# Expert stage: the experts of the last 32 first keys computed densely, the others gathered by row

## The chip, the cores and the metric

The program runs on one core of one Trainium2 chip, in one launch. The metric is device time in microseconds (us); all arithmetic is float32 (parts of the GEMMs split a float32 operand in two). The core has a matrix engine (TensorE, in the profile PE, its weight loads PEld), three others for elementwise work (VectorE, DVE; ScalarE, ACT; GpSimd, POOL), SyncE (SP), which here only issues loads and stores, and sixteen DMA engines. POOL issues the gathers by row.

## The reference, cut to what matters

Two transformer blocks run one after the other on x of 256 tokens by 2048 columns. The change lies in the last part of the second block, a layer with 16,384 experts of one row each, of which every token uses 16 in each of 8 heads:

```python
q = (hf @ wq).reshape(T, PEER_HEADS, 2, PEER_DQ // 2)          # T = 256, 8 heads, 2 halves of 128
s = jnp.einsum('thpd,hpkd->thpk', q, keys)                     # 128 keys in each half
v1, i1 = lax.top_k(s[:, :, 0], 16);  v2, i2 = lax.top_k(s[:, :, 1], 16)
cand = v1[..., :, None] + v2[..., None, :]                     # 256 candidates
cidx = i1[..., :, None] * 128 + i2[..., None, :]               # expert = first key * 128 + second key
vals, pick = lax.top_k(cand, 16)
eidx, g = cidx[pick], softmax(vals)
act = gelu(einsum('td,thkd->thk', x_c, down[e_c])) * g_c       # down, up: 16384 x 2048
out = einsum('thk,thkd->td', act, up[e_c])                      # sum over heads and picks
```

The result is x + gt2 * out, where gt2 is one row of 2048 factors made from the conditioning vector. There are 256 * 8 * 16 = 32,768 picks. The first key of an expert is its index divided by 128.

## The kernel before, in words

Everything up to the expert stage is a chain of GEMMs with weights streamed in 1 MB pieces; nothing there changes. At its end, `hf` holds the normalized input, transposed (2048 features on 16 chunks of 128 partitions, 256 tokens along a row), `xN` the residual in the same layout, `htok` both token halves with tokens on partitions, and `gB` gt2 on all partitions. Instructions go through a helper that records all of them under line 94; the gathers are the exception (line 1600). From line 1528 on the order on each engine is chosen by a planner, which plays the program in a model of time; where it is free it follows the order of the code.

The stage's wq GEMM runs first. Work is then cut in 16 items: token half `qt` (128 tokens) by head `hd`. For each item:

- `route` (line 1557): two small matmuls against the keys, then top 16 of each half, top 16 of the 256 sums and their indices on DVE; result: expert indices `ei` and gates `g`, one row per token, one column per pick.
- `downs` (1603): for each of 16 picks, POOL gathers 128 rows of `down` (one per token, 8 KB each, 1 MB) into a tile `dn`, and DVE multiplies it with `htok` and sums it to one column of `dots`.
- the loop from line 1642: `cf` = gelu(dots) * g. For each pick, a gather of 128 rows of `up`, ACT puts the column of `cf` on a diagonal (`cdg`, 128 x 128), and four matmuls with it as weights add the 128 x 2048 tile, scaled by row, to four PSUM banks `acc`. The gathers of the next item's `dn` alternate with this item's `up`. The last two items do 14 of their rows on DVE instead (`side`).

After head 7 of a half, `acc` is multiplied by `gB`, added to the residual (`x3t`, tokens on partitions, made by 16 transposes) and stored.

Tiles of 8 KB per partition come from one pool of 14 (`unit`); `dn`, `htok`, `pq` (the wq result), `hf`, `xN`, `gB` and `keysT` share it. The tiles of `up` have eight buffers of another pool, in which GEMM weights were before. POOL issues gathers in order; each waits for its buffer.

Of the kernel before, what the change touches and what calls it, by code (L numbers as in the profile page):

```python
# [10 lines left out]
F32 = mybir.dt.float32  # L11
F32R = mybir.dt.float32r
I32 = mybir.dt.int32
# [7 lines left out]
P = 128  # L21
# [7 lines left out]
NCMP = 15  # L29


def _consts():
# [29 lines left out]
    for j in range(512):  # L62
# [7 lines left out]
    return {"cst_a": csta, "cst_b": cstb.astype(f), "cst_c": hot}  # L70
# [5 lines left out]
        "do": 5.0, "ro": 0.0, "nf": 3, "tail": 2}  # L76
# [3 lines left out]
def tile_kernel(ctx: ExitStack, tc: tile.TileContext, I, out):  # L80
# [1029 lines left out]
    def gt2_bcast():  # L1110
        acc = unit([P, D], "gB")
        yield from ada_acc(2, 5, acc)
        br = wp.tile([1, D], F32, name=nm("gb"), tag="W")
        SY.dma_start(br, I["ada_b_2"][:, 5 * D:6 * D])
        for q in range(4):
            sl = slice(512 * q, 512 * q + 512)
            ps = pmisc([P, 512], "gbp")
            T.matmul(ps, ones, acc[:, sl], start=True, stop=False)
            T.matmul(ps, ones[0:1, :], br[:, sl], start=False, stop=True)
            S.copy(acc[:, sl], ps)  # L1120
            yield 0.0
        mods["gB"] = acc

    queue_ada(*later[TUNE["nf"]:])
# [403 lines left out]
    pinned[0] = False  # L1528

# [16 lines left out]
    htok = [unit([P, D], "htok") for _ in range(2)]  # L1546
    down, upw = I["peer_down_2"][0], I["peer_up_2"][0]
    gB = mods["gB"]
# [7 lines left out]

    def route(qt, hd):
        ps = pmisc([P, 2, P], "ksc")
# [23 lines left out]
        ee = tiny([P, 2, 16], "ee")  # L1582
        for a in range(2):
            oh_ = scr([P, 16, 16], "oh")
            V.tensor_tensor(oh_, pf[:, 1 + a, :].unsqueeze(2).to_broadcast([P, 16, 16]),
                            iota16.unsqueeze(1).to_broadcast([P, 16, 16]), OP.is_equal)
            V.tensor_tensor(oh_, oh_, ixf[:, a, :].unsqueeze(1).to_broadcast([P, 16, 16]), OP.mult)
            V.tensor_reduce(ee[:, a, :], oh_, axis=AX.X, op=OP.add)
        V.scalar_tensor_tensor(ee[:, 0, :], ee[:, 0, :], 128.0, ee[:, 1, :], op0=OP.mult, op1=OP.add)
        ei = tiny([P, 16], "eid", I32)  # L1590
        V.tensor_copy(ei, ee[:, 0, :])
# [4 lines left out]
        V.tensor_scalar(g[:, 0:16], g[:, 0:16], g[:, 18:19], None, op0=OP.mult)  # L1596
        return ei, g

    def gather(rows_, table, idx):
        G.indirect_dma_start(out=rows_, out_offset=None, in_=table,  # L1600
                             in_offset=bass.IndirectOffsetOnAxis(ap=idx, axis=0))

    def downs(it):
        qt, hd, ei, g, dots = it
        for k in range(16):
            rt = unit([P, D], "dn")
            gather(rt, down, ei[:, k:k + 1])
            V.scalar_tensor_tensor(rt, rt, 1.0, htok[qt], op0=OP.mult, op1=OP.mult,
                                   accum_out=dots[:, k:k + 1])
            yield 2.2  # L1610

    def item(i):
        qt, hd = divmod(i, 8)
        ei, g = route(qt, hd)
        return qt, hd, ei, g, tiny([P, 16], "dots")

    def by_token():
        yield from hf_shift()
        for t in range(2):
            yield from tokens(hf, htok[t], t)  # L1620
# [6 lines left out]
    for nn in (256, 256, 512, 512, 512):  # L1627
# [6 lines left out]
        if c0 == 0:  # L1634
            dgen.append(downs(items[0]))
            stream.append(dgen[0])
# [3 lines left out]
    x3t = unit([P, D], "x3t")  # L1640
    side = None
    for i in range(16):
        qt, hd, ei, g, dots = items[i]
        if hd == 0:
            acc = [pacc_([P, 512], "pe") for _ in range(3)] + [pmisc([P, 512], "pe")]
        if i + 2 < 16:
            items.append(item(i + 2))
        cf = tiny([P, 16], "cf")
        S.activation(cf, dots, AF.Gelu)
        V.tensor_mul(cf, cf, g[:, 0:16])  # L1650
        nxt = downs(items[i + 1]) if i + 1 < 16 else iter(())
        for k in range(16):
            next(nxt, None)
            rt = rot_tile("up")
            gather(rt, upw, ei[:, k:k + 1])
            if i >= 16 - TUNE["tail"] and k % 2 == 0 and k < 14:

                if side is None:
                    side = unit([P, D], "side")
                    V.tensor_scalar(side, rt, cf[:, k:k + 1], None, op0=OP.mult)  # L1660
                else:
                    V.scalar_tensor_tensor(side, rt, cf[:, k:k + 1], side, op0=OP.mult, op1=OP.add)
                continue
            dg = scr([P, P], "cdg")
            S.activation(dg, ident, AF.Copy, scale=cf[:, k:k + 1])
            for n in range(4):
                T.matmul(acc[n], dg, rt[:, 512 * n:512 * n + 512], start=(hd == 0 and k == 0),
                         stop=(hd == 7 and k == 15), skip_group_check=True)
        for _ in nxt:
            pass  # L1670
        if hd == 5:
            for _ in tokens(xN, x3t, qt):
                pass
        if hd == 7:
            if side is not None:
                V.tensor_mul(side, side, gB)
                V.tensor_add(x3t, x3t, side)
            for n in range(4):
                sl = slice(512 * n, 512 * n + 512)
                o = scr([P, 512], "o")  # L1680
                V.tensor_mul(o, acc[n], gB[:, sl])
                V.tensor_add(o, o, x3t[:, sl])
                SY.dma_start(out[0, qt * P:(qt + 1) * P, sl], o)
# [24 lines left out]
```

## Time and profile before

| | |
|---|---|
| median of 3 runs | 3374.34 us (3374.03 to 3379.35) |
| the profiled execution | 3373.42 us, span from first to last instruction 3371.5 us |
| mean granted clock of PE | 0.938 |
| busy in the span: PE, DVE, ACT, POOL | 88%, 68%, 30%, 24% |
| gathers of `dn` and of `up` | 256 each |
| moved in all | 1068.19 MB, 538.26 MB of it on POOL's queue |

The profile is of one execution. Busy shares are of the whole span: three fifths of it, up to about 2050 us, are GEMMs with PE nearly full, and the expert stage comes after. A row of a group gives line, engine, operation, the tile written and those read, the count, then the busy time together, the mean of one instruction, the idle time of its engine just before, and what ended it.

### The profile page before, as it was taken

To read this page: it belongs to the slowest core of one execution; us is meant where nothing else is said; L and a number is where in the kernel's file an instruction comes from. 1 tells how busy PE (TensorE), PEld (TensorE's weight loads), DVE (VectorE), ACT (ScalarE), POOL (GpSimd) and SP (SyncE) were. 2 spreads that over 40 slices of the span, in tenths; PEclk is the share of its full clock that TensorE was granted. 3 is DMA by queue.
4 is the path that set the end of the run, shared out by engine and by line. 5 is a ranking of instruction groups with operands and counts; after the bars stand their busy time and mean duration, and the time that the engine had idled before them with its cause. 6 is when DMAs were issued, how large, how long until landed. Compare 5 with 4: busy or idle time off the path is not lost.

```text
span 3371.5 us, 44165 instructions
## 1 busy us (share of the span) xinstructions
PE 2971.9 (88%) x18020; PEld 2298.6 (68%) x18020; DVE 2302.0 (68%) x3363; ACT 1024.8 (30%) x1364; POOL 793.1 (24%) x540
## 2 busy tenths in 40 slices
PE   6899999999999999999999997877787678677777
PEld 2687889999999999999999997433333233223333
DVE  7687779876778778765876659655655566664735
ACT  1323433444444444444346653111111101111100
POOL 1000000000000000000000003666665566664654
PEclk8899999999999999999999998988888889888888
DMA  9866567876899989874783438999999999999998
GB/s 367 301 218 218 200 236 243 307 264 216 294 332 330 325 320 325 320 250 161 264 270 121 147 113 321 416 421 422 422 421 421 421 420 422 421 421 405 422 393 360
DMA packets 280401, 1068.19 MB, mean 317 GB/s; under 512 B 27428, under 2 KB 36039, under 8 KB 189573
## 3 DMA queue, kind: packets, MB, share of 16 engines
q1 hardware_dynamic: 202370, 524.35, 44.5%
q0 software_dynamic: 74752, 538.26, 38.7%
q10 hardware_dynamic: 3076, 2.76, 0.3%
q8 instruction: 141, 2.31, 0.3%
q14 instruction: 62, 0.51, 0.0%
HBM read 1063.19 MB, written 2.11 MB: 316 GB/s over the span
## 4 chain that ended last, share of the span: by engine, by line
PE 64%; DMA 24%; DVE 5%; issue 4%; POOL 3%; ACT 0%; SPq 0%; POOLq 0%; DVEq 0%; ACTq 0%
PE ga L94 48%; DMA up<-in_peer_up_dram,eid 12%; DMA dn<-in_peer_down_dram,eid 11%; PE pe L94 6%; PE gb L94 2%; DMA aw<-in_w_ada_dram 2%; POOL up L1600 2%; POOL dn L1600 2%; DVE dn L94 2%; PE adap L94 1%; PE bu L94 1%; PE rms L94 1%; PE yp L94 1%; PE o L94 1%; PE sc L94 0%
## 5 line engine op out<-in xcount | busy, mean ns | idle before, releaser
L94 PE MATMUL pe<-up,cdg 128*128 128x512 f32 x1936 | 920.7, 637 | 310.1 <-DMA up<-in_peer_up_dram,eid 189.1
L94 PEld LDWEIGHTS pe<-up,cdg 128*128 128x128 f32 x1936 | 390.1, 205 | 833.1 <-issue 621.2
L1600 POOL DMA_INDIRECT dn<-in_peer_down_dram,eid x256 | 394.5, 1541 | 2246.6 <-DVE g L94 1998.0
L94 DVE TENSOR_TENSOR wl<-w,wh 128x2048 fp32r<-128x2048 f32 (+2 forms) x304 | 680.6, 2239 | 316.8 <-ACT wh L94 265.4
L94 ACT ACTIVATE wh<-w 128x2048 fp32r<-128x2048 f32 (+2 forms) x304 | 570.0, 1875 | 882.3 <-PE ga L94 738.1
L94 DVE SCALAR_TENSOR_TENSOR dn<-dn,htok 128x2048 f32<-128x2048 f32 x256 | 583.1, 2288 | 326.2 <-DMA dn<-in_peer_down_dram,eid 325.7
L1600 POOL DMA_INDIRECT up<-in_peer_up_dram,eid x256 | 385.6, 1506 | 274.5 <-PE pe L94 98.8
L94 DVE SCALAR_TENSOR_TENSOR acc<-aw,cT,acc 128x2048 f32<-128x2048 f32 x105 | 246.3, 2346 | 22.8 <-DMA aw<-in_ada_w_dram 13.6
L94 PE MATMUL ga<-h2h,wh 128*128 128x256 f32 x1024 | 250.0, 285 | 4.1 <-ACT h2h L94 4.1
L94 PE MATMUL ga<-h2l,wh 128*128 128x256 f32 x1024 | 249.5, 284 | 0.2 <-DVE h2l L94 0.2
L94 PE MATMUL ga<-ah,wh 128*128 128x256 f32 x1024 | 249.3, 283 | 0.0
L94 PE MATMUL ga<-al,wh 128*128 128x256 f32 x1024 | 249.0, 283 | 0.0
L94 ACT ACTIVATE cdg<-ca,cf 128x128 f32<-128x128 f32 x242 | 84.9, 394 | 489.1 <-PE pe L94 462.0
L94 PE MATMUL ga<-h1h,wh 128*128 128x256 f32 x896 | 224.1, 289 | 0.0
L94 PE MATMUL ga<-h1l,wh 128*128 128x256 f32 x896 | 220.5, 285 | 0.0
L94 PEld LDWEIGHTS ga<-h2h,wh 128*128 128x128 f32 x1024 | 197.3, 193 | 6.1 <-ACT h2h L94 4.4
L94 PEld LDWEIGHTS ga<-h2l,wh 128*128 128x128 f32 x1024 | 197.1, 193 | 0.5 <-DVE h2l L94 0.5
L94 PEld LDWEIGHTS ga<-ah,wh 128*128 128x128 f32 x1024 | 196.5, 192 | 0.8 <-ACT wh L94 0.8
L94 PEld LDWEIGHTS ga<-al,wh 128*128 128x128 f32 x1024 | 196.5, 192 | 0.0
L94 PEld LDWEIGHTS ga<-h1h,wh 128*128 128x128 f32 x896 | 172.8, 193 | 19.5 <-issue 15.3
L94 PEld LDWEIGHTS ga<-h1l,wh 128*128 128x128 f32 x896 | 173.0, 193 | 0.9 <-issue 0.8
L94 PE MATMUL ga<-h3h,wh 128*128 128x256 f32 x528 | 133.4, 291 | 1.1 <-ACT h3h L94 1.1
(443 smaller groups left out, 4568.1 us busy)
## 6 DMA issues: line engine op xcount, KB each, us to landing
w<-in_w_ff_dram SPq DMA_DIRECT2D x128, 1024.0 KB, 5.8
w<-in_w_in_dram SPq DMA_DIRECT2D x100, 1024.0 KB, 5.3
aw<-in_w_ada_dram SPq DMA_DIRECT2D x96, 1024.0 KB, 6.8
aw<-in_ada_w_dram SPq DMA_DIRECT2D x96, 1024.0 KB, 5.7
w<-in_w_out_dram SPq DMA_DIRECT2D x32, 1024.0 KB, 5.2
w<-in_peer_wq_dram SPq DMA_DIRECT2D x12, 1024.0 KB, 5.2
w<-in_w_proj_attn_dram SPq DMA_DIRECT2D x8, 1024.0 KB, 5.1
w<-in_w_proj_ssm_dram SPq DMA_DIRECT2D x8, 1024.0 KB, 5.4
```

The lines of the kernel that those rows point to most:

```text
L94: r = f(*a, **k)
L1600: G.indirect_dma_start(out=rows_, out_offset=None, in_=table, in_offset=bass.IndirectOffsetOnAxis(ap=idx, axis=0))
```

## The change

Experts of first keys 96 to 127 (4,096 of 16,384) are taken out of the gathers: an index of 12,288 or more is over a bound given with the indirect DMA, and such a row is left as it was in the tile. Their part is computed for all 256 tokens, as three steps interleaved with the 16 items by a generator `dense` that `pump` advances 2.5 us of credit per pair of gathers: (1) for each of 32 first keys, load 128 rows of `down`, transpose them, multiply with `hf`, gelu into `A` (experts on partitions, tokens along the row); (2) for 16 tokens at a time, build one-hot matrices of first and second key on DVE, multiply them on PE to gates by expert and token, and scale `A` with them; (3) multiply `A` with the rows of `up`, in four column blocks.

The `up` sum also changes shape. A gathered tile no longer holds one pick of 128 tokens but four picks of 32 tokens (`by_rows` rearranges indices and coefficients by 16 small ACT copies each), and is multiplied by a 128 x 32 matrix of coefficients (`wq4`), so that its sums go to 32 of the 128 output partitions; two tiles with different output partitions are taken in turn. All routing is done by the end of item 7. `xN` goes to DRAM and back (`xdr`), gt2 is kept there as one row, the second half's `htok` is made at item 6, and the first half's sums are evicted to `held` and stored with the dense part of the end.

```diff
+MD = 32
+LO = P - MD
-        "do": 5.0, "ro": 0.0, "nf": 3, "tail": 2}
+        "do": 5.0, "ro": 0.0, "nf": 3, "pd": 2.5}
@@ gt2_bcast
-        mods["gB"] = acc
+        SY.dma_start(gdr, acc[0:1, :])
+        mods["gB"] = gdr
@@ before the wq GEMM
+    for i in range(2):
+        SY.dma_start(xdr[i], xN[i].rearrange("p a t -> p (a t)"))
+    quad = flip[:, 0:32]        # sum of the four column blocks of the identity
...
     def gather(rows_, table, idx):
         G.indirect_dma_start(out=rows_, out_offset=None, in_=table,
-                             in_offset=bass.IndirectOffsetOnAxis(ap=idx, axis=0))
+                             in_offset=bass.IndirectOffsetOnAxis(ap=idx, axis=0),
+                             bounds_check=LO * P - 1, oob_is_err=False)
...
+    def by_rows(src, copy, name, dt=F32):
+        dst = tiny([P, 4, 4], name, dt)
+        sv = src.rearrange("p (q s) -> p s q", s=4)
+        for sl in range(4):
+            for j in range(4):
+                copy(dst[32 * sl:32 * sl + 32, j, :], sv[32 * j:32 * j + 32, sl, :])
+        return dst
+    def dense():
+        for c in range(MD):
+            if c % 8 == 0:
+                A.append(unit([P, 8, L], "act"))
+            dl = unit([P, D], "dl")
+            SY.dma_start(dl, down[(LO + c) * P:(LO + c + 1) * P, :])
+            ps = pmisc([P, L], "ds")
+            for q in range(4):
+                pt = pmisc([P, 4, P], "dt")
+                for k in range(4):
+                    T.transpose(pt[:, k, :], dl[:, (4 * q + k) * P:(4 * q + k + 1) * P], ident)
+                dT = scr([P, 4, P], "dT")
+                S.copy(dT, pt)
+                for k in range(4):
+                    kc = 4 * q + k
+                    T.matmul(ps, dT[:, k, :], hf[kc // 8][:, kc % 8, :], start=(kc == 0), stop=(kc == NC - 1))
+                yield 2.25
+            S.activation(A[-1][:, c % 8, :], ps, AF.Gelu)
+        while len(items) < 16 or not gb:
+            yield None
+        for qt in range(2):
+            ...                  # sel[qt]: first key, second key, gate by pick -> transposed to st
+            for t0 in range(0, P, 16):
+                goh = scr([P, 16, MD], "goh")
+                V.tensor_tensor(goh, st[:, 0, t0:t0 + 16]..., iota[:, LO:P]..., OP.is_equal)
+                V.tensor_tensor(goh, goh, st[:, 2, t0:t0 + 16]..., OP.mult)
+                pg = pmisc([P, 16, MD], "pg")
+                for q in range(4):
+                    oh2 = scr([P, 4, P], "oh2")
+                    V.tensor_tensor(oh2, st[:, 1, t0 + 4 * q:t0 + 4 * q + 4]..., iota..., OP.is_equal)
+                    for k in range(4):
+                        T.matmul(pg[:, 4 * q + k, :], oh2[:, k, :], goh[:, 4 * q + k, :], start=True, stop=True)
+                    yield 1.0
+                for u in range(MD // 8):
+                    V.tensor_mul(a, a, pg[:, :, 8 * u:8 * u + 8]...)   # a: 16 tokens of A[u]
+        for n in range(4):
+            pd = [pmisc([P, 512], "pd") for _ in range(2)]
+            for c in range(MD):
+                if c % 4 == 0:
+                    ut = unit([P, 4, 512], "ut")
+                    SY.dma_start(ut, upw[(LO + c) * P:(LO + c + 4) * P, sl]...)
+                for t in range(2):
+                    T.matmul(pd[t], A[c // 8][:, c % 8, t * P:(t + 1) * P], ut[:, c % 4, :], ...)
+                yield 1.9
+            ...                  # times gB, added to x3t; first half stored
+    def up_tile():
+        tag = "WHLWWHLW"[turn_[0] % 8]
...
     for i in range(16):
+        for _ in range((14 * (i + 1)) // 8 - (14 * i) // 8 if i < 8 else 0):
+            items.append(item(len(items)))
+        er = by_rows(sel[qt][:, 3, own], S.copy, "er", I32)
+        V.scalar_tensor_tensor(gm, sel[qt][:, 0, own], LO - 0.5, sel[qt][:, 2, own], op0=OP.is_lt, op1=OP.mult)
+        V.memset(cf, 0.0)
+        V.copy_predicated(cf, gm.bitcast(U32), dots)
+        S.activation(cf, cf, AF.Gelu)
+        V.tensor_mul(cf, cf, gm)
+        cr = by_rows(cf, S.copy, "cr")
+        V.tensor_mul(wq4, quad..., cr...)
-        for k in range(16):
-            ...
-            dg = scr([P, P], "cdg")
-            S.activation(dg, ident, AF.Copy, scale=cf[:, k:k + 1])
-            for n in range(4):
-                T.matmul(acc[n], dg, rt[:, 512 * n:512 * n + 512], ...)
+        for q, jj in [(q, jj) for q in range(4) for jj in ((0, 1), (2, 3))]:
+            for j in jj:
+                next(nxt, None)
+                rts[j] = up_tile()
+                gather(rts[j], upw, er[:, j, q:q + 1])
+                if i >= 8:
+                    next(gres, None)
+                pump(TUNE["pd"])
+            for n in range(4):
+                for j in jj:
+                    T.matmul(acc[n][32 * j:32 * j + 32, :], wq4[:, 4 * j + q, :],
+                             rts[j][:, 512 * n:512 * n + 512], ...)
```

`gres` steps the generator that reads `xdr` back, transposes it to `x3t` and spreads gt2 from DRAM to all partitions.

## Rows read from the trace of the kernel before

**Rows 1.** Windows: us; busy (count) PE, PEld, DVE, ACT, POOL; PEclk, DMA share, GB/s
```profile
2100.00:3371.50 1271.50, 949.53 (x2164) 418.78 (x2164) 727.01 (x1082) 141.32 (x338) 756.30 (x497) 0.87 1.00 412
2200.00:3100.00 900.00, 662.78 (x1435) 284.46 (x1436) 507.19 (x822) 100.08 (x246) 539.57 (x356) 0.86 1.01 421
...
3300.00:3371.50 71.50, 50.01 (x107) 20.62 (x105) 37.86 (x29) 3.28 (x10) 25.61 (x17) 0.90 0.84 349
```
**Rows 2.** DMA, 2200 to 3100 us: queue's packets, MB, share; issues, us to landing
```profile
q0 software_dynamic: 51860, 377.67, 100.9%
...
dn<-in_peer_down_dram,eid POOLq DMA_INDIRECT x183, 19.1
```
**Rows 3.** Chain of waits, start us and us (one of some 40 alike)
```profile
2234.74 19.12 DMA dn<-in_peer_down_dram,eid
```
**Rows 4.** Groups of instructions, 2100 us to the end
```profile
L94 PE MATMUL pe<-up,cdg 128*128 128x512 f32 x1936 | 920.7, 637 | 310.1 <-DMA up<-in_peer_up_dram,eid 189.1 <-ACT cdg L94 106.5 <-ACT cf L94 14.5
L94 DVE SCALAR_TENSOR_TENSOR dn<-dn,htok 128x2048 f32<-128x2048 f32 x246 | 560.3, 2288 | 323.8 <-DMA dn<-in_peer_down_dram,eid 323.4
...
L1600 POOL DMA_INDIRECT up<-in_peer_up_dram,eid x254 | 382.4, 1506 | 273.9 <-PE pe L94 98.8 <-DMA up<-in_peer_up_dram,eid 66.2 <-DMA dn<-in_peer_down_dram,eid 64.9
L1600 POOL DMA_INDIRECT dn<-in_peer_down_dram,eid x243 | 373.9, 1539 | 223.7 <-DMA dn<-in_peer_down_dram,eid 78.1 <-DMA up<-in_peer_up_dram,eid 49.1 <-issue 42.9
```
**Rows 5.** Windows: 8 KB rows of w_ada; 2 KB weight pieces; the wq GEMM
```profile
60.00:80.00 20.00, 16.86 (x89) 6.15 (x87) 17.49 (x94) 5.77 (x10) 0.00 (x0) 0.82 1.01 421
1700.00:1800.00 100.00, 100.00 (x816) 97.89 (x815) 75.19 (x155) 45.58 (x61) 0.00 (x0) 1.00 0.72 242
2000.00:2050.00 50.00, 49.55 (x392) 49.12 (x392) 39.31 (x86) 35.37 (x57) 5.07 (x4) 0.94 0.66 227
```
**Rows 6.** Timeline of PE, merged runs: start us, us; three GEMM stretches, then expert stage
```profile
191.02 1.06 PE L94 MATMUL adap<-aw,crep 128*32 128x512 f32 x8
206.77 1.48 PE L94 MATMUL yp<-p,bct 128*32 128x256 f32 x10
1808.38 0.81 PE L94 MATMUL pr<-cu,gw 128*128 128x256 f32 x3
3204.76 7.46 PE L94 MATMUL pe<-up,cdg 128*128 128x512 f32 x17
```
**Rows 7.** Groups on PE over the span: transposes; 15-column matmuls
```profile
L94 PE MATMUL tok<-ca,x 128*128 128x128 f32 x32 | 5.1, 283 | 3.6 <-ACT x3t L94 2.0 <-ACT scs L94 1.6
L94 PE MATMUL cs<-kcn,q 128*128 128x15 f32 x32 | 3.8, 254 | 0.0
```
**Rows 8.** Timeline of POOL near 3255 us: start us, us
```profile
3252.23 0.94 POOL L1600 DMA_INDIRECT dn<-in_peer_down_dram,eid  x1 [0.30 <-issue]
3259.42 2.16 POOL L1600 DMA_INDIRECT dn<-in_peer_down_dram,eid  x1 [0.30 <-issue]
3261.88 2.20 POOL L1600 DMA_INDIRECT dn<-in_peer_down_dram,eid  x1 [0.30 <-issue]
```
**Rows 9.** Timeline of DVE in the same stretch
```profile
3258.47 2.29 DVE L94 SCALAR_TENSOR_TENSOR dn<-dn,htok 128x2048 f32<-128x2048 f32 x1 [0.16 <-DMA dn<-in_peer_down_dram,eid]
3260.69 0.08 DVE L94 DVE_READ_ACCUMULATOR dn<-dn,htok 128x1 f32 x1
```
**Rows 10.** Groups of small instructions, 2100 us to the end
```profile
L94 DVE TENSOR_TENSOR o<-pe,gB 128x512 f32<-128x512 f32 x8 | 5.2, 682 | 4.8 <-PE pe L94 4.8
L94 DVE MAX8 v<-scs 128x8 f32<-128x128 f32 x26 | 6.3, 284 | 92.6 <-ACT scs L94 92.6
L94 ACT ACTIVATE cf<-dots 128x16 f32<-128x16 f32 x16 | 3.5, 216 | 338.8 <-DVE dn L94 338.8
```
**Rows 11.** End of the chain of waits
```profile
3347.40 8.97 DMA up<-in_peer_up_dram,eid
...
3367.05 1.20 DVE o L94 x2
```

More of the change, by code (lines that the diff above doesn't have):

```diff
@@ L1544, in tokens @@
             yield 0.5
-    htok = [unit([P, D], "htok") for _ in range(2)]
+    htok = [unit([P, D], "htok"), None]
     down, upw = I["peer_down_2"][0], I["peer_up_2"][0]
-    gB = mods["gB"]
     def top16(vals, idx, src, w):
@@ L1555, in top16 @@
         V.max_index(idx[:, 8:16], vals[:, 8:16], rest)
+    sel = [scr([P, 4, P], "sel") for _ in range(2)]
     def route(qt, hd):
+        own = slice(16 * hd, 16 * hd + 16)
         ps = pmisc([P, 2, P], "ksc")
@@ L1613, in item, with with_dots @@
         qt, hd = divmod(i, 8)
-        ei, g = route(qt, hd)
-        return qt, hd, ei, g, tiny([P, 16], "dots")
+        route(qt, hd)
+        return qt, hd
+    def with_dots(it):
+        return (*it, tiny([P, 16], "dots"))
     def by_token():
         yield from hf_shift()
-        for t in range(2):
-            yield from tokens(hf, htok[t], t)
+        yield from tokens(hf, htok[0], 0)
     start(by_token())
@@ new lines, in tile_kernel, with pump, residual_rows @@
+    gdense = dense()
+    dcred = [0.0]
+    def pump(us):
+        dcred[0] += us
+        while dcred[0] > 0:
+            v = next(gdense, None)
+            if v is None:
+                dcred[0] = 0.0
+            else:
+                dcred[0] -= v
+    def residual_rows():
+        g_ = unit([P, D], "gB")
+        a = gdr[0:1, 0:1]
+        SY.dma_start(g_, bass.AP(tensor=a.tensor, offset=a.offset, ap=[[0, P], [1, D]]))
+        xs = [unit([P, 8, L], "xs") for _ in range(2)]
+        for i in range(2):
+            SY.dma_start(xs[i].rearrange("p a t -> p (a t)"), xdr[i])
+        for t in range(2):
+            x3t.append(unit([P, D], "x3t"))
+            for _ in tokens(xs, x3t[t], t):
+                yield
+        gb.append(g_)
@@ new lines, in tile_kernel @@
+        if i == 6:
+            htok[1] = unit([P, D], "htok")
+            for _ in tokens(hf, htok[1], 1):
+                pass
+        er = by_rows(sel[qt][:, 3, own], S.copy, "er", I32)
+        gm = tiny([P, 16], "gm")
+        V.scalar_tensor_tensor(gm, sel[qt][:, 0, own], LO - 0.5, sel[qt][:, 2, own], op0=OP.is_lt, op1=OP.mult)
+        cf = tiny([P, 16], "cf")
+        V.memset(cf, 0.0)
+        V.copy_predicated(cf, gm.bitcast(U32), dots)
+        S.activation(cf, cf, AF.Gelu)
+        V.tensor_mul(cf, cf, gm)
@@ L1670, in tile_kernel @@
             pass
-        if hd == 5:
-            for _ in tokens(xN, x3t, qt):
-                pass
[L1674 to L1677, printed above, removed]
+        if i == 8:
+            for _ in gres:
+                pass
+            for n in range(4):
+                sl = slice(512 * n, 512 * n + 512)
+                V.tensor_mul(held[n], held[n], gb[0][:, sl])
+                V.tensor_add(x3t[0][:, sl], x3t[0][:, sl], held[n])
+            done[0] = True
@@ L1678, in tile_kernel @@
+        if hd == 7 and qt == 0:
+            held_ = unit([P, 4, 512], "held")
+            held = [held_[:, n, :] for n in range(4)]
+            for n in range(4):
+                S.copy(held[n], acc[n])
+        if i == 15:
+            pump(1e9)
             for n in range(4):
```

99 lines of the change are left out of this document (66 added, 33 removed).

## The prediction

> **What bounds the kernel now.** I read the stage windows first. From 2100 us to the end the DMA engines are full and no compute engine is: DMA share 1.00 against PE 75%, DVE 57%, POOL 59% [rows 1]. From 2200 to 3100 the rate stands still at 421 GB/s, and the queue table says what fills it: the software queue with the gathered rows takes 100.9% of sixteen engines [rows 1, 2]. A gather lands 19.1 us after its issue, though one ends every 2.49 us (1.049 MB at 421 GB/s): about eight are in flight [rows 2]. The chain of waits agrees: its long pieces are "DMA dn" and "DMA up" of 19 us with a POOL issue between them [rows 3]. So the expert stage is its bytes: 512 gathers x 1.049 MB = 536.9 MB, at 421 GB/s 1275 us, of a span of 3371.5 us.
>
> The other engines by group: the up matmuls keep PE busy for 921 us, the dot products DVE for 560 us, the issues POOL for 756 us (1.51 and 1.54 us each) [rows 4].
>
> **The change part by part.**
>
> *Rows not gathered.* The reference, evaluated on its own inputs, sends 7,327 of the 32,768 (token, expert) picks to first keys 96 to 127: 22.4%, from 16% to 32% by head and token half. If such a row costs no transfer, both tables lose 2 x 7,327 x 8 KB = 120.0 MB, at 421 GB/s **-285 us**. If the skipped rows are moved all the same, 0. The trace has no gather with a bound; I take the full saving, since the rate is set by bytes.
>
> *Dense loads.* 32 blocks of the down table, 33.6 MB in rows of 8 KB: such loads also reach 421 GB/s at a full DMA share [rows 5], 80 us. The up table's 33.6 MB come in 2 KB pieces as the GEMM weights do: 242 GB/s at share 0.72 is 336 at full share [rows 5], 100 us (between 80 by the 8 KB rate and 105). xdr read back and gB spread, 3.1 MB: 7 us. Together **+187 us**. The xdr write (2 MB, 5 us, on SP's queue ahead of the last wq pieces) and the gdr store fall where the DMA share is 0.66 and PE has GEMM work: 0, at most 5. Net DMA: 1275 - 285 + 187 = 1177 us, **-98 us**. Spread over 512 gathers that is 2.30 us each.
>
> *PE.* Its instructions are recorded as two passes. Full-width passes of 512 columns follow each other at 0.43 us (17 in 7.46), of 256 columns at 0.215 (three in 0.81, the last one's tail included) [rows 6]. With 32 output partitions and different column groups, passes run side by side: four groups put 8 passes of 512 into 1.06 us, two groups 10 passes of 256 into 1.48, 0.14 instead of 0.215 [rows 6]. The new up step has two groups in turn, so 2,048 passes at half of 0.43: 440 us (881 if they do not pair). Dense down: 512 transposes at 0.16 (32 in 5.1 [rows 7]) and 1,024 passes at 0.215, 302 us; selection: 512 passes of 32 columns at 0.12 (from 32 in 3.8 with 15 columns), 61 us [rows 7]; dense up: 512 passes at 0.43, 220 us. With routing some 1,035 us at full clock, below 1177; at the mean granted clock of before, 0.87 with PE idle a quarter of the time, 1,190 [rows 1]; PE is idle less now, and I expect more than 0.95 of full speed. PE gets near the bound without being it: 0.
>
> *DVE.* The dots stay 256 x 2.37 us (2.29 and the read of 0.08 [rows 9]); the 14 routes of the loop (some 10 us each: DVE's 727 us less the dots' 580 [rows 1, 4]) move into the first eight items, where they and the dots fill about 443 of the 575 us of DMA; by items that is bursty but covered by the row buffers: 0 to +15 with the next part. The selection phase is different. For each 16 tokens it has two 128x512 products and four 128x512 comparisons at 0.68 and four 128-element products at 0.28 (by rows of the same widths) [rows 10]: 5.2 us, 16 times, 83 us. Its 64 yields of credit 1.0 are pumped at 2.5 per gather pair, so in some 26 pairs, whose dots add 61 us: 144 us of DVE against 26 x 2 x 0.814 MB / 421 GB/s = 100 us of DMA. DVE is the bound there, and less dense loading lies beside it. Five buffered rows give back about 12 us: **+33 us** (bounds 0, if the scheduler spreads it, and 45).
>
> *POOL.* The number of gathers stays. A gather with DVE idle takes 0.94 us of POOL, with 0.30 before the next; with dot products on DVE it takes 2.16 to 2.20 [rows 8], and the two views side by side show why: the gather begun at 3259.42 ends at 3261.58, 0.8 us after the end of the dot product that ran when it began [rows 8, 9]. The mean pitch is 1.52 + 0.30 = 1.82 us (539.57 us by 356 gathers [rows 1]); 2.30 is needed. DVE gets busier (57% to about 73%), so the mean rises towards 2.1: still hidden, no longer by much. The test of the bound is unknown: 0 to 0.3 us, hidden too.
>
> The Trainium skill, SBUF — State Buffer, section "SBUF: two separate sides", says that VectorE with two SBUF inputs and a GpSimd instruction that reads SBUF exclude each other for a whole instruction. The trace agrees: the dot product has two SBUF inputs, and the gather beside it takes 2.16 us, not 0.94 [rows 8, 9]. That rule speaks against this change; what it would do is the second rival below.
>
> *Buffers and uneven rows.* The unit pool stays at 14. At items 6 and 7 pq (2), keysT, hf (2), htok (2) and A (4) hold eleven, and three are left for dot rows and dense blocks together, where five were left to dot rows. That stretch lasts some 20 pairs (90 us); I allow a tenth to a quarter of it. A skipped row also leaves some DMA engines less to do than others in a gather. Neither shows in the trace: 0 to +45 us, I take **+20**.
>
> *Item boundaries.* Coefficients now pass 16 small ACT copies and a 128x512 product: 16 x 0.2 (the 0.216 of a 16-column activation [rows 10]) + 0.7, some 5 us more after the last dot. Eight up buffers hold 8 x 2 x 1.94 = 31 us of DMA work with the dots between: hidden. Evicting acc after item 7 and the residual's transposes lie beside DMA: 0.
>
> *End.* Before, the last gather lands at 3356.4 and the program ends 15 us later [rows 11]; the DMA share of the last 71 us is 0.84 [rows 1]. Dense credit is 288 + 64 + 243 = 595; its second and third part wait for gB (item 8, pair 9 or so), then 119 pairs x 2.5 = 298 of 307 are pumped, and 9 us of matmuls stay for the end: the last pair 1.7, 9, products and sums 8, the store 5: 24 us, +9, and 3 lost earlier in the last item, which has no dots to load: **+12 us** (0 to 30).
>
> Sum: -98 + 33 + 20 + 12 = -33 us. The profiled execution took 3373.42 us, 1.9 over its span, 0.9 under the median shown: 3373.4 - 33 = **3340 us**.
>
> **Rivals.**
> 1. *DMA stays full throughout.* The selection phase and the buffers cost nothing, as queue depth hides routing today [rows 1]; -98 + 12: 3288 us. Against it: 144 us of DVE in a stretch of 100.
> 2. *Descriptor issue becomes the bound: slower.* Place: POOL beside DVE. If each gather pays the locked pitch of 2.18 + 0.30 = 2.48 us [rows 8], the gathers take 512 x 2.48 = 1270 us however many rows they skip; with the three terms above the sum is -5 + 65: 3433 us. In part, at a mean pitch of 2.40, 3373 - 33 + 51 = 3391. It decides from a mean of 2.30 + 33/512 = 2.36 on: there the 33 us of the forecast are gone. For it: DVE busier, new instructions with two SBUF inputs, nearly every gather meeting one. Against: 1.82 today at 57%. I set 3400.
> 3. *Skipped rows cost their transfer time:* 1275 + 187, +187 plus some of the other terms hidden: 3560 us. For it only that no row shows a bound.
> 4. *Column groups do not pair:* PE has 1,035 + 441 = 1,476 us, 201 more than the 1275 of today's DMA; with the end, 3373 + 201 + 12 = 3586 us. Against it both rows of column groups [rows 6].
>
> **How the numbers follow.** Forecast 0.44 (its own range 3310 to 3366), rival 1 0.16, rival 2 0.27, rival 3 0.08, rival 4 0.05. A difference under 0.2% (7 us) can't be told from none. Faster: 0.41 of the forecast and all of rival 1, 0.57. Same: 0.03 of the forecast and 0.05 of rival 2, 0.08. Slower: the rest, 0.35. The range of 3280 to 3440 leaves out 3 and 4 (0.13) and the edges of 1 and 2 (0.06).
>
> **What would show it.** Right: gathers' bytes in the stage near 417 MB, DMA share about 0.95 with a dip where the selection comparisons run, up passes starting in pairs, PE near 90% there, the mean POOL pitch under 2.3. Wrong: 537 MB gathered (rival 3); DMA share under 0.9 with POOL instructions of 2.2 us back to back (rival 2); PE never idle (rival 4). The forecast falls if a stretch outside the selection phase has DMA below 0.9 for more than 50 us, or if the dip is missing.

## The result, and the profile after

The changed kernel takes 3614.81 us (median of four runs, 3602.20 to 3624.82), the kernel before beside it 3374.74 (3374.03 to 3379.35): ratio 1.0706, 95% interval 1.0671 to 1.0742. It is 240 us slower; the forecast was 34 faster, and the time lies above the range. The profiled execution took 3612.45 us with a span of 3610.7.

Windows of the changed kernel (us; busy and count of PE, PEld, DVE, ACT, POOL; PEclk, DMA share, GB/s), first the stretch of [rows 1], then the items that carry the routing, the later items, and what follows the last dot product:

```profile
2200.00:3100.00 900.00, 689.03 (x3122) 397.45 (x3121) 516.95 (x1036) 173.24 (x556) 410.81 (x304) 0.86 0.80 309
...
2110.00:2795.00 685.00, 552.49 (x2444) 321.53 (x2444) 351.20 (x722) 147.10 (x422) 277.72 (x220) 0.91 0.79 308
2795.00:3527.00 732.00, 562.04 (x2051) 243.31 (x2052) 399.36 (x565) 68.03 (x307) 382.46 (x264) 0.84 0.87 341
...
3527.00:3610.70 83.70, 71.21 (x220) 23.41 (x218) 10.85 (x19) 3.32 (x17) 7.91 (x8) 0.93 0.41 145
```

No engine is full, and DMA no longer is: 0.80 where [rows 1] have 1.01. The DMA view of the changed kernel (GB/s in 40 slices of 2100 to 3600 us, then packets, queue and landing times of 2200 to 3100) shows how it falls:

```profile
GB/s 365 411 169 409 390 160 410 305 258 315 216 387 315 270 326 220 337 309 177 374 418 329 383 248 408 302 274 406 273 371 331 336 412 305 410 252 409 384 256 45
...
DMA packets 48136, 278.25 MB, mean 309 GB/s; under 512 B 13763, under 2 KB 13763, under 8 KB 14347
q0 software_dynamic: 43314, 246.07, 70.1%
...
up<-in_peer_up_dram,er POOLq DMA_INDIRECT x155, 9.8
dn<-in_peer_down_dram,eid POOLq DMA_INDIRECT x149, 12.0
```

The rate is not evenly low but a sawtooth, full for a slice or two and then down to 160 to 270: something empties the queue once an item. A gather lands after 9.8 to 12.0 us, not 19.1 [rows 2]; with 304 gathers in 900 us, one in 2.96 us, that is three to four in flight where there were eight. The same by the three windows above: 0.79 x 685 + 0.87 x 732 + 0.41 x 83.7 = 1,212 us of transfer, and 289 of idleness; with the 10 us ahead of them 1,222 of 1,511. Before, DMA was busy for all of its 1,271.5 [rows 1]. So 50 us of transfer were saved and 289 of idleness added.

Groups of the changed kernel, 2100 us to the end (busy, mean ns of one | idle just before, and what ended it), the first four against [rows 4]:

```profile
L97 DVE SCALAR_TENSOR_TENSOR dn<-dn,htok 128x2048 f32<-128x2048 f32 x244 | 552.5, 2289 | 533.7 <-DMA dn<-in_peer_down_dram,eid 490.5 <-issue 24.1 <-PE pe L97 12.7
L97 PE MATMUL pe<-up,wq 128*32 128x512 f32 x2048 | 544.1, 621 | 126.1 <-DVE wq L97 114.9 <-DMA up<-in_peer_up_dram,er 11.2
L1616 POOL DMA_INDIRECT up<-in_peer_up_dram,er x256 | 360.5, 1408 | 441.2 <-PE pe L97 200.9 <-ACT er L97 164.2 <-issue 47.1
L1616 POOL DMA_INDIRECT dn<-in_peer_down_dram,eid x240 | 317.5, 1323 | 346.6 <-DVE eid L97 112.3 <-DVE dn L97 91.4 <-issue 50.0
L97 PE MATMUL ds<-hf,dT 128*128 128x256 f32 x1024 | 254.4, 402 | 89.3 <-ACT dT L97 89.3
L97 PE MATMUL pd<-ut,act 128*128 128x512 f32 x512 | 246.5, 635 | 59.1 <-DMA ut<-in_peer_up_dram 59.1
L97 PE MATMUL pg<-goh,oh 128*128 128x32 f32 x512 | 79.2, 323 | 7.1 <-DVE goh L97 7.1
L97 PE MATMUL dt<-ca,dl 128*128 128x128 f32 x512 | 70.7, 280 | 26.4 <-DMA dl<-in_peer_down_dram 17.2 <-ACT scs L97 9.1 <-ACT htok L97 0.2
```

The waits that matter are POOL's, since it issues the gathers: before an `up` gather it waits 201 us for PE to free a buffer and 164 for the indices `er`; before a `dn` gather 112 for the index cast and 91 for a dot product. Four timelines of the changed kernel show one item boundary (start us, us; in brackets the idle time before). DVE:

```profile
2384.17 2.29 DVE L97 SCALAR_TENSOR_TENSOR dn<-dn,htok 128x2048 f32<-128x2048 f32 x1 [2.68 <-DMA dn<-in_peer_down_dram,eid]
2386.38 2.29 DVE L97 SCALAR_TENSOR_TENSOR dn<-dn,htok 128x2048 f32<-128x2048 f32 x1
...
2395.88 2.29 DVE L97 SCALAR_TENSOR_TENSOR dn<-dn,htok 128x2048 f32<-128x2048 f32 x1 [0.59 <-DMA dn<-in_peer_down_dram,eid]
2398.10 0.08 DVE L97 DVE_READ_ACCUMULATOR dn<-dn,htok 128x1 f32 x1
2402.50 0.49 DVE L97 MAX8 v<-scs 128x8 f32<-128x128 f32 x2 [4.32 <-ACT scs L97]
...
2415.07 0.16 DVE L97 COPY_PREDICATED cf<-gm,dots 128x16 f32<-128x16 uint32 x1
...
2417.32 0.17 DVE L97 CAST eid<-sel 128x16 int32<-128x16 f32 x1
...
2420.66 0.69 DVE L97 TENSOR_TENSOR wq<-ca,cr 128x512 f32<-128x512 f32 x1 [1.45 <-ACT cr L97]
```

ACT:

```profile
2407.69 3.31 ACT L97 CAST er<-sel 32x4 int32<-32x4 f32 x16
...
2416.90 0.22 ACT L97 ACTIVATE cf<-cf 128x16 f32<-128x16 f32 x1
2417.36 3.28 ACT L97 COPY cr<-cf 32x4 f32<-32x4 f32 x16 [0.24 <-DVE cf L97]
```

POOL:

```profile
2384.45 2.87 POOL L1616 DMA_INDIRECT dn<-in_peer_down_dram,eid  x1 [0.30 <-issue]
2387.63 1.91 POOL L1616 DMA_INDIRECT dn<-in_peer_down_dram,eid  x1 [0.31 <-issue]
2410.62 0.99 POOL L1616 DMA_INDIRECT up<-in_peer_up_dram,er  x1 [21.09 <-ACT er L97]
...
2420.97 1.24 POOL L1616 DMA_INDIRECT dn<-in_peer_down_dram,eid  x1 [0.30 <-issue]
```

PE, with the dense block (`ds`, `dt`) and the score matmuls of the two routings (`ksc`):

```profile
2399.08 1.99 PE L97 MATMUL ds<-hf,dT 128*128 128x256 f32 x8 [0.68 <-ACT dT L97]
2400.91 0.60 PE L97 MATMUL dt<-ca,dl 128*128 128x128 f32 x4
2401.35 1.06 PE L97 MATMUL ksc<-keysT,pq 128*128 128x128 f32 x8
```

The item's last dot product starts at 2395.9. Its coefficients depend on nothing else, yet their matrix `wq` is made at 2420.7: two routings stand ahead of them on DVE (2402 to 2417), and ACT has both `er` and `cr` to copy between. The routings start only there, after their score matmuls, which run on PE at 2401 in the midst of the dense work. POOL, whose last `dn` gather ended at 2389.5, issues nothing for 21 us. From the start of the last dot product to `wq` it is 21 us on average over the first eight items (8 to 31), and 6.3 in each of the last eight, which have no routing.

### The profile page after: what moved, and what is told of

Its sections match the earlier page's. It is cut to its first block, busy times and chain, and to the rows that moved or that the text cites. A ratio compares the mean times of both kernels' runs of the same rounds, so it can differ in the third digit from the quotient of the medians.

```text
span 3610.7 us, 50720 instructions
## 1 busy us (share of the span) xinstructions
PE 3221.4 (89%) x20698; PEld 2484.9 (69%) x20698; DVE 2347.1 (65%) x3590; ACT 1108.7 (31%) x1790; POOL 718.8 (20%) x540
## 2 busy tenths in 40 slices
DMA packets 302802, 1021.06 MB, mean 283 GB/s; under 512 B 43203, under 2 KB 51942, under 8 KB 221860
## 3 DMA queue, kind: packets, MB, share of 16 engines
q0 software_dynamic: 74752, 418.28, 29.4%
## 4 chain that ended last, share of the span: by engine, by line
PE 71%; DMA 11%; DVE 7%; issue 6%; ACT 2%; POOL 2%; POOLq 0%; SPq 0%; ACTq 0%; DVEq 0%
PE ga L97 45%; PE pe L97 8%; DMA dn<-in_peer_down_dram,eid 6%; PE ds L97 5%; DMA up<-in_peer_up_dram,er 3%; PE gb L97 2%; PE pd L97 2%; DVE dn L97 2%; DMA aw<-in_w_ada_dram 2%; PE adap L97 1%; POOL dn L1616 1%; PE dt L97 1%; POOL up L1616 1%; PE pg L97 1%; PE bu L97 1%
## 5 line engine op out<-in xcount | busy, mean ns | idle before, releaser
L1616 POOL DMA_INDIRECT dn<-in_peer_down_dram,eid x256 | 345.3, 1349 | 2368.9 <-DVE eid L97 2106.2
L97 PE MATMUL pe<-up,wq 128*32 128x512 f32 x2048 | 544.1, 621 | 126.1 <-DVE wq L97 114.9
L97 PEld LDWEIGHTS pe<-up,wq 128*32 128x32 f32 x2048 | 139.6, 113 | 491.1 <-issue 363.8
L1616 POOL DMA_INDIRECT up<-in_peer_up_dram,er x256 | 360.5, 1408 | 441.2 <-PE pe L97 200.9
L97 PE MATMUL ds<-hf,dT 128*128 128x256 f32 x1024 | 254.4, 402 | 89.3 <-ACT dT L97 89.3
L97 PE MATMUL pd<-ut,act 128*128 128x512 f32 x512 | 246.5, 635 | 59.1 <-DMA ut<-in_peer_up_dram 59.1
L97 PEld LDWEIGHTS ds<-hf,dT 128*128 128x128 f32 x1024 | 198.2, 200 | 140.9 <-ACT dT L97 96.7
L97 PEld LDWEIGHTS pd<-ut,act 128*128 128x128 f32 x512 | 100.4, 202 | 204.8 <-issue 137.3
```

What stands on the lines that cost most here:

```text
L97: r = f(*a, **k)
```

## The experiments

Each ran beside the kernel before. All, with the ratio to it:

| kernel | median us | ratio | 95% interval |
|---|---|---|---|
| e1 indices ahead | 3618.89 | 1.0723 | 1.0705 to 1.0740 |
| e2 all rows moved | 3741.69 | 1.1084 | 1.1066 to 1.1103 |
| e3 before, late index | 3380.09 | 1.0016 | 1.0007 to 1.0026 |
| e4 no dense part | 3157.33 | 0.9355 | 0.9337 to 0.9374 |
| e5 routes in item | 3512.63 | 1.0414 | 1.0395 to 1.0432 |
| e6 dense, loaded once | 3688.25 | 1.0928 | 1.0906 to 1.0950 |
| e7 dense loads only | 3406.43 | 1.0093 | 1.0073 to 1.0113 |
| e8 four buffers held | 3290.58 | 0.9750 | 0.9730 to 0.9769 |
| e9 four groups | 3479.33 | 1.0314 | 1.0296 to 1.0331 |
| e10 half the matmuls | 3466.30 | 1.0270 | 1.0249 to 1.0290 |
| e11 more row buffers | 3492.78 | 1.0348 | 1.0327 to 1.0369 |
| e12 16 keys, credit 1.4 | 3401.33 | 1.0086 | 1.0065 to 1.0106 |
| e13 16 keys, four groups | 3358.33 | 0.9952 | 0.9936 to 0.9969 |
| e14 e13, row buffers | 3372.00 | 0.9990 | 0.9981 to 1.0000 |
| e15 8 keys, four groups | 3356.77 | 0.9945 | 0.9929 to 0.9962 |
| e16 16 keys, order of the change | 3458.47 | 1.0248 | 1.0231 to 1.0265 |
| e17 16 keys, two groups | 3366.29 | 0.9977 | 0.9968 to 0.9987 |
| e18 no dense part, routes in item | 3139.75 | 0.9309 | 0.9293 to 0.9324 |

The first theory (A) was what POOL's waits say: the indices come late. Its rivals were the rows themselves, the dense part's bytes, its PE work and its buffers, and (D) the coefficients, late behind the routing.

**e1, indices ahead.** Both index tiles are made right behind each item's routing:

```diff
     def item(i):
         route(qt, hd)
+        V.tensor_copy(eis[qt, hd], ix)
+        ers[qt, hd] = by_rows(ix, S.copy, "er", I32, ...)
-        er = by_rows(sel[qt][:, 3, own], S.copy, "er", I32)
+        er = ers[qt, hd]
```

> The changed kernel with both index tiles (eid for dn, er for up) made right after each item's routing, into free columns of an old constant tile, instead of at the item's boundary. Theory A (indices late: POOL waits 164 us for er in eight items and 112 us for eid in seven, and the DMA queue drains each time): most of these 276 us go, 3614.8 falls to 3340 to 3430. Theory B (PE is the bound, because dense matmuls and up matmuls stand in one order): less than 40 us, 3575 to 3615. Theory C (DMA bytes are the bound in spite of its lower share): unchanged.

No gain. POOL's waits of e1 (us, times, longest) show why:

```profile
POOL up L1616 <- PE pe L97: 303.1, 72, 31.6
POOL dn L1616 <- DVE dn L97: 226.4, 41, 17.7
```

No wait on an index is left, but of its 276 us 237 stand again as waits for buffers (303.1 + 226.4 against 200.9 + 91.4): the gathers go out a little earlier and then stop, since the tiles ahead of them are used up only when the coefficients come. Theory A, as the single cause, falls, although it named the two largest new waits. The run is not a clean price of late indices, though: its edit also made the coefficients later, on average 34 us from the last dot product to `wq` in the first eight items, against 21 in the change.

**e3, the kernel before with the index cast at the start of the dot products.**

```diff
-        ei = tiny([P, 16], "eid", I32)          # in route
-        V.tensor_copy(ei, ee[:, 0, :])
+        ei = tiny([P, 16], "eid", I32)          # in downs
+        V.tensor_copy(ei, ee[:, 0, :])
```

> The kernel before with one edit: the cast of the expert index is made at the start of the item's dn gathers, as in the changed kernel, instead of in the routing two items ahead. Theory A: each of 15 boundaries drains the dn gathers for some 8 to 16 us, 3374 rises by 100 to 240 us. Theories B and C: no change (within 10 us).

5 us. POOL does wait for the cast here (us, times, longest):

```profile
POOL dn L1598 <- DVE eid L94: 98.3, 11, 19.4
```

DMA stays at 1.00 from 2200 to 3100: with eight gathers in flight a late index is nearly free.

**e2, no row skipped.** The bound is put above all indices:

```diff
-                             bounds_check=LO * P - 1, oob_is_err=False)
+                             bounds_check=P * P - 1, oob_is_err=False)
```

> The changed kernel with the bound raised to 16383, so that no row is skipped; the extra rows get weight 0 as before. 120 MB more are moved, 285 us at 421 GB/s. Theory A (DMA idles at every boundary): part of it is hidden in the idle time, +60 to +200 us. Theory B (PE): under +60. Theory C (DMA): +250 to +290. If skipped rows cost their transfer time all along: 0.

127 us over the changed kernel, for 120 MB more. Skipping saves transfer time, and part of the saving is lost in idleness; rival 3 falls.

**e4, without the dense part:**

```diff
-                pump(TUNE["pd"])
-            pump(1e9)
```

> The changed kernel without the dense part (no dense loads, transposes, matmuls or selection; the sums of the experts of the last 32 first keys are missing). DMA left in the stage: 417 MB, 990 us, against 1177. Theory A: the boundaries stay and only the dense part's own DMA and stalls go: 3350 to 3480. Theory B: PE is free, DMA full: 3374 - 285 = 3080 to 3150. Theory C: 3612 - 187 = 3425.

Window of e4, the stretch of [rows 1]:

```profile
2200.00:3100.00 900.00, 504.20 (x1806) 143.76 (x1804) 591.35 (x960) 116.11 (x504) 680.72 (x435) 0.76 0.99 392
```

DMA is full again and the gain is there, 217 us. So the dense part alone costs 3614.8 - 3157.3 = 457 us, against 187 of loads and 65 of side effects in the prediction. And a full queue moves 392 GB/s here, not 421.

**e8 and e7, the dense part taken apart.** e8 is e4 with four unit tiles held idle through the loop; e7 has the change's loads and tiles and none of their work on PE, DVE and ACT.

```diff
+    kept = [unit([P, D], "kept") for _ in range(4)]     # e8, read once at the end
```

> e4 (no dense part) with four tiles of the unit pool held idle through the stage, as A holds them in the changed kernel. Theory E (row buffers): 3157 rises by 60 to 250 us. Theories B and D: under 40 us.

> The changed kernel with the dense loads, and the tiles A, dl, ut and hf held as long as before, but no dense work on PE, ACT or DVE (the sums of the dense experts are missing). 67 MB more than e4's DMA, 187 us. Theory B: 3157 + 187 = 3345, at most 3380. Theory E (buffers): 3450 to 3600.

Window of e8:

```profile
2200.00:3100.00 900.00, 402.99 (x1612) 114.49 (x1612) 531.60 (x898) 108.09 (x456) 573.98 (x384) 0.72 0.89 349
```

The main wait of POOL that is new in e8 (us, times, longest) is this:

```profile
POOL dn L1616 <- DVE eid L97: 146.0, 13, 19.4
```

In e4 the same wait is 3.0 us. So the late index that e3 found nearly free is what POOL waits for once four tiles are gone; e8 with an early index was not run. Four held tiles and nothing else cost 133 us; the loads add 116, less than their transfer time, since they fall into idleness that is there; the work on PE, DVE and ACT adds the last 208. 133 + 116 + 208 = 457. The split holds in this order of adding only, and it is coarse: e7 also holds `dl`, `ut` and `hf`, its coefficients come 12 us after the last dot product in the first eight items (6.5 in e8), and at 3406 it lies in the range of neither theory.

**e6, dense work on one loaded block** (one `dl` and one `ut` tile for all):

```diff
-            dl = unit([P, D], "dl")              # and its load
+            if c == 0:
+                dl = unit([P, D], "dl")          # and its load; ut in the same way
```

> The changed kernel with all dense work, but one block of down and one of up loaded for all (the output's dense part is that of the wrong experts): 65 MB less is loaded, 180 us of DMA, and dense blocks take two buffers in all. Theory B (PE work in its order): 3560 to 3615. Theory E (buffers and loads): 3200 to 3350, near the 3157 of e4. Theory C (DMA bytes): 3612 - 180 = 3435.

A miss: 65 MB less and 73 us slower than the change, DMA share 0.64 from 2200 to 3100. It says that bytes aren't the bound; but it also keeps two more tiles busy and lets the dense work run without its own waits, and which of the two costs more it can't tell.

**e5, the coefficients ahead of the routing.** e1, with each routing moved from ahead of the item's coefficients to the middle of its gathers:

```diff
-        for _ in range((14 * (i + 1)) // 8 - (14 * i) // 8 if i < 8 else 0):
-            items.append(item(len(items)))
...
         for q, jj in ...:
+            if (q, jj[0]) in ((0, 2), (2, 2)) and more:
+                more -= 1
+                items.append(item(len(items)))
```

> Run e1 (indices ahead) with the routing of later items moved from the head of an item to its middle, behind the item's coefficients in program order. In e1 PE waits 129 us for wq, ten times, because coefficients stand behind one or two routings on DVE and ACT. Theory D (the coefficients' delay holds PE, PE holds the up buffers, these hold POOL): 3619 falls by 80 to 150 us. Theory B (PE has too much to do in one order): under 40 us. Theory E (too few row buffers): under 40 us.

106 us come back without one instruction less. Window of e5:

```profile
2200.00:3100.00 900.00, 743.38 (x3321) 422.30 (x3320) 557.28 (x1076) 197.88 (x610) 465.89 (x321) 0.87 0.87 335
```

`wq` now follows the start of the last dot product by 6 to 11 us in every item (item 4: 2460.6 and 2467.6), 8 us on average in the first eight items against 34 in e1 and 21 in the change. Theory D holds for this part. Against the change itself, which has the indices late as well, e5 gains 102. The other half of the loss stays: 3512.6 is still 138 over before.

**e9, e10, e11: what is left, one candidate each on top of e5.** Four `up` tiles in turn instead of two; every second dense matmul left out; two `up` buffers given to `dn`:

```diff
-        for q, jj in [(q, jj) for q in range(4) for jj in ((0, 1), (2, 3))]:
+        for q, jj in [(q, (0, 1, 2, 3)) for q in range(4)]:                    # e9
...
-                for k in range(4):
+                for k in range(0, 4, 2):            # e10, and pd for even c only
...
-            rt = unit([P, D], "dn")
+            rt = wp.tile(..., tag="H", bufs=2) if k % 3 == 1 else unit([P, D], "dn")   # e11, in the loop
```

> Run e5 with the up sums taken over four tiles in turn, one for each of the four column groups, instead of two and two. The up step's PE time falls from 2,048 passes at 0.215 us (440) to 2,048 at 0.125 (256, by the four-group rows of the kernel before). Theory F (with coefficients in time, PE is the bound in the phases with dense matmuls: 16 x (1.7 + 2.4) us an item at full clock): 3513 falls by 60 to 150 us. Theory E (buffers): it rises, since four of eight up buffers come free together: 0 to +60.

> Run e5 with every second matmul of the dense down step and of the dense up step left out (the dense experts' sums are then partial); loads, transposes, tiles and order stay. PE is relieved of 110 + 110 us. Theory F: 3513 falls by 80 to 200 us. Theory E: under 40 us.

> Run e5 with two of the eight up buffers given to dn: six for up, and one in three dn tiles from the two. e8 put the price of four buffers held at 133 us without dense work. Theory E: 3513 falls by 30 to 100 us. Theory F: no gain, 0 to +40 because PE holds the up buffers longer.

-33, -46 and -20 us: each gain is clear of the noise and below the range that its theory gave, and none carries the rest. In e11 the coefficients come later again (13 us on average in the first eight items), so its 20 is not the price of the buffers alone. Half of the dense matmuls (200 us of PE by the groups) buy 46.

**e12, e16, e17, e13: half the dense part.** All have `MD = 16`. e12 is e5 so cut, with credit 1.4 a pair; e17 the same with 1.8; e16 is the changed kernel with 1.8, order and all; e13 is e17 with e9's four groups.

```diff
-MD = 32
+MD = 16
-"pd": 2.5
+"pd": 1.8          # e12: 1.4
```

> Run e5 with the last 16 first keys dense instead of 32, pumped at 1.4 instead of 2.5: half the dense loads (94 us of DMA less), half the dense matmuls, two tiles of A instead of four; about half of the skipped rows are gathered again (some 140 us of DMA more). If DMA bytes were the limit it would rise by 40 to 60 us. Theories E and F: it falls to 3400 to 3460.

> Kernel: the changed kernel with 16 dense first keys and credit 1.8 and nothing else moved: routing ahead of the coefficients, indices late, two groups. Against e13 it prices the order and the groups with half the dense work. Theory D (order matters by itself, since the coefficients wait behind routing whatever the dense work is): 80 to 130 us over e13, 3440 to 3480. Theory F (only the sum of dense work over buffers matters): the order costs half of its 106, 3390 to 3420.

> Kernel: e13 with two column groups in turn instead of four (so e16 with the routing in mid-item and the indices ahead, and e12 with credit 1.8). It prices the order alone and the groups alone at half the dense work. If order is a cost by itself (theory D): 90 to 110 us under e16, 3350 to 3370, and e13's groups gave about nothing. If it is a cost that needs the dense work beside it (theory F): half of 106, so 3395 to 3410, and the groups gave the other 40.

> Kernel: e12 (16 dense first keys, routing in mid-item) with the up sums over four tiles in turn as in e9, and credit 1.8 so that the dense work ends before the last item's gathers. If the losses of the dense part are PE time and order on top of half-size loads (theory D and E together), the four groups give half of what they gave in e9 (-33) and the shorter tail gives 30 of the 94 us: 3340 to 3365, just faster than before. If what is left in e12 is the four held buffers and a gather rate that the small rows lower (theory F, no PE), the groups change nothing and it stays at 3380 to 3400.

Windows of e16, then of e13:

```profile
2200.00:3100.00 900.00, 639.79 (x2610) 305.17 (x2611) 549.42 (x1040) 140.62 (x512) 496.09 (x344) 0.82 0.91 370
```
```profile
2200.00:3100.00 900.00, 662.26 (x2770) 304.64 (x2774) 588.08 (x1094) 156.58 (x553) 541.93 (x357) 0.82 0.98 395
```

With half the dense part, indices and order together cost 92 us (e16 to e17), nearly the 102 of the whole (the change to e5); the four groups give 8. From e12 to e17, where only the credit differs, 35 us are gained: e12 leaves more dense work for the end, and 94 us pass there after the start of its last dot product, in e17 47.

**e18, the order without the dense part**, e4 with e5's edit:

> Kernel: e4 (no dense part, its sums are missing from the output) with the routing in mid-item and the indices ahead, as in e5. Theory D (order is a cost by itself): e4's DMA share is already 0.97 to 1.0, so at most 10 to 20 us come back, 3135 to 3150; the cost shows only where the queue has no reserve. If it gains 50 or more, the order was a cost without any dense work. If it is the same as e4 within 5 us, the order costs only through the buffers that the dense part takes.

18 us, as theory D had it, but not as the price of late coefficients with a full queue, since e4 has none. One of its boundaries on DVE:

```profile
2317.84 2.28 DVE L97 SCALAR_TENSOR_TENSOR dn<-dn,htok 128x2048 f32<-128x2048 f32 x1
...
2320.71 0.25 DVE L97 CAST eid<-sel 128x16 int32<-128x16 f32 x1
...
2324.14 0.69 DVE L97 TENSOR_TENSOR wq<-ca,cr 128x512 f32<-128x512 f32 x1 [3.18 <-ACT cr L97]
```

`wq` follows the last dot product by 6.3 us in 15 of e4's 16 items, and in e8 too; the routings are done between earlier dot products, though they stand ahead of the coefficients in the code. In the change it takes 21 us in the first eight items, in e16 14. So the code's order becomes a delay only together with the dense work, and the 102 and 92 us were measured only there. What the same delay would cost with eight gathers in flight, no run shows; e3 and e8 show it for the index alone.

**e14 and e15, towards a faster version.** e14 is e13 with e11's buffers, e15 has `MD = 8` and credit 1.2:

> Kernel: e13 with two up buffers given to the down rows in the loop, as in e11. Where e11 gave -20 with 32 dense keys, here only two A tiles are held: if the buffers of the down rows still bind, -10 to -20 against e13; if two held tiles cost nothing, the six up buffers left make it 0 to +15.

> Kernel: e13 with 8 dense first keys and credit 1.2: a quarter of the dense work, one A tile, and 7,327 skipped rows cut to about a quarter. The DMA work alone is then 71 us less for rows and 50 more for loads. If the dense part's losses scale with its size, 3345 to 3365; if each part has a fixed cost (sixteen small copies, the residual read back, the tail), about 3370 or more.

e14 is 14 us slower than e13: with two tiles of `act` instead of four, the `up` buffers may be worth more where they were, but the coefficients also come later (13 us on average, 6.5 in e13), and which of the two it is was not separated. e13 and e15 beat both kernels, by 0.5% (ratios 0.9952 and 0.9945, intervals in the table). e13 moves 1042.56 MB in all and e15 1060.04, before 1068.19: 61 and 19 us less at 421 GB/s, for 16 and 17 gained. The ends, from the start of the last dot product, are also shorter than before (46 us in e13, 58 in e15, 63 before), so the runs do not say how much of either gain comes from bytes.

## Why the prediction was wrong

**The steps that failed: "Item boundaries: hidden" and the +20 of "Buffers and uneven rows".** Both rest on one assumption, that the queue keeps its reserve (the tiles whose gathers are in flight). I counted eight `up` buffers as 31 us of cover at a boundary and set the added coefficient work, 5 us, against it. Left out were the two routings that the loop now puts between the last dot product and the coefficients, two at a time in most of the first eight items (the prediction moved their DVE time and not their place), and that the `up` gathers wait there for `er`, so that the eight buffers stand empty while they should cover. In these items the coefficients followed the start of the last dot product by 8 to 31 us, where they take 6.3 without routing. Measured: 102 us from the change to e5, which moves indices and routings out of the way (106 of it against e1). The held tiles were taken to matter for some 90 us of the run, +20; four of them held throughout cost 133 (e8; the change takes its four one after another in the first six items). The two belong together: with the reserve, 98 us of POOL's waits for an index cost 5 us of time (e3); with four tiles gone, POOL waits 146 us for the index and the queue falls to 0.89 (e8). That late coefficients behave alike is argued from this, not measured.

**Rows not gathered: bytes right, size off.** Predicted -285. Packets of the gathers fell by 120.0 MB (538.26 to 418.28 MB on POOL's queue), as worked out. But the full queue of e4 moves 392 GB/s, so that e4 gains 217, not 285; the rate of 421 was taken over from gathers that moved every row.

**Dense loads.** +187 of transfer was sized as if it displaced gathers. With the four tiles already held they cost 116 (e7 less e8, the tiles of the loads included).

**PE, "near the bound without being it: 0".** The total was right: 544 + 254 + 247 + 79 + 71 = 1,195 us in the groups, 1,190 predicted at the old clock; the clock stayed at 0.86, where I expected over 0.95. The column groups pair (2,048 records of 621 ns make only 544 us of busy time), and rival 4 falls. The error is in the use: an average over 1,177 us says nothing on an item in which PE has the dense block, the `up` passes and a wait for `wq` of up to 26 us one behind the other. Half of the dense matmuls are worth 46 us (e10), not 0.

**DVE's selection phase.** 144 us of DVE were predicted, and its stretch has this window in the changed kernel:

```profile
2925.00:3105.00 180.00, 145.84 (x750) 94.10 (x751) 146.62 (x239) 13.59 (x68) 103.44 (x67) 0.74 0.84 319
```

The work is as sized, though a dot product and its read take 2.30 us and not 2.37, since the read starts before the dot product's end [rows 9]. There is no dip: DMA at 0.84 lies between 0.81 in the 130 us before and 0.90 in what follows, so +33 can't be told apart here. In e13, with half the dense keys, DMA is 0.94 in the stretch (2770 to 2960 us) against 0.99 on both sides, an estimated 10 us of idleness: the effect exists where the queue is otherwise full.

**POOL: 0, right.** Gathers take 1.41 and 1.32 us on average and POOL is busy for 676 us of 1,510. Rival 2 had the sign and not the mechanism. One gather beside a dot product takes 1.91 to 2.87 us, ending 0.9 us after the dot product that ran when it began, and alone 0.99 (DVE and POOL timelines above); that agrees with the rule of the Trainium skill, SBUF — State Buffer, section "SBUF: two separate sides", on instructions that exclude each other, which decides nothing where POOL waits for buffers.

**End: +12, too small.** From the start of the last dot product to the end of the program it is 83 us, before 63: +20, inside the 0 to 30 that was given. The chain of waits of the changed kernel shows the kind of it (start us, us):

```profile
3533.69 0.70 DVE wq L97
3534.44 5.29 PE pe L97 x16
3539.72 1.92 PE pd L97 x4
3541.64 3.56 PE pe L97 x16
3545.20 5.35 PE pd L97 x12
...
3591.63 3.56 PE pe L97 x16
3595.19 4.50 PE pd L97 x10
```

The last item has no gathers of `dn` to hide behind, and PE works off `up` pairs and the dense remainder in turn, with DMA at 0.41. I had counted 9 us of matmuls behind the last pair, and not that those pumped within the item stand on the same path.

The sum in the end: DMA transfer about -50 instead of -98, idleness +289 instead of +65. "DMA below 0.9 outside the selection phase for more than 50 us" was named as what would refute the forecast, and it is what happened. What stays open: of e5's 138 us over before, e9 to e11 name parts of 33, 46 and 20 that were measured one at a time; whether they add up at 32 keys was not run. Nor was e8 with an early index, or the delay of the coefficients with a full reserve.

## What to carry to other kernels

This stage ran at full DMA rate by its reserve of tiles in flight (e4 at 0.99 and e8 at 0.89 differ in four tiles): before taking tiles from that pool or putting work between the last input and its consumer, count the reserve as landing time over pitch, and price the boundary without it. A wait that the profile names largest can be the first of several that end together; e1 removed 276 us of waits and no time, while its edit lengthened another delay. So look in the trace of every run whether the edit changed only what it was meant to, and whether the thing that it removes was there at all: e18 took away an order that in e4 did not delay the coefficients. When extra work is to be hidden, put what frees buffers (here the coefficients) first in every engine's program order, and cut the extra work until the bound engine is full again.

## What the runs showed of the hardware

- A row over the bound still makes a packet: the changed kernel has 74,752 packets on POOL's queue, as many with every row moved (e2), and with the skip 14,654 more of them under 512 bytes (43,203 against 28,549). In the packet records such a one takes 9 ns; a moved row of 8 KB takes 316 ns on average before, 325 in e4 and 329 in the change.
- A full queue (share 0.99) moves 392 GB/s in e4, where 22% of the rows are skipped, and 421 (share 1.01) in [rows 1]; why a moved row takes longer there the runs do not show.
- The landing time of a gather goes with the number in flight, worked out as landing time over pitch: 19.1 us with eight [rows 2], 12 with five (e8, 384 gathers in 900 us), 9.8 to 12.0 with three to four in the change.
